# A third place for the low parts of layer 0's queries, and layer 1's attention with its low value product last, its loads asked for one head ahead, and its side work begun earlier

## The chip, the cores and the metric

The kernel runs on one core of one Trainium2 chip. The metric is the device time of one execution in microseconds (us). Five engines work beside each other, each with its own queue of instructions, and they wait for each other by semaphores: PE (TensorE, matrix products; its weight loads are listed apart as PEld), ACT (ScalarE), DVE (VectorE), POOL (GpSimd) and SP (SyncE), which here issues every DMA.

## The reference

The reference is a trunk of two layers over 2048 tokens of width 1024, batch 1, in float32.

- **Layer 0** normalises, multiplies by one combined input matrix and runs two attentions: mixer A (8 query heads and 2 key heads of width 64, a window of own plus two previous 64-token chunks, a learned sink, rotary) and mixer B (8 heads of width 64, own plus eight previous chunks, a learned relative bias). Each output is multiplied by a SiLU gate; both are joined, go through one output matrix and are added to the residual.
- **Layer 1** normalises, multiplies by one input matrix (queries, keys, values, gate) and runs mixer C, differential attention: 8 heads, each with two query and key maps of width 64 and values of width 128, causal by 64-token chunk:

```
s1 = q1 @ k1.T / 8 ; s2 = q2 @ k2.T / 8          # masked by chunk
a  = softmax(s1) - lam * softmax(s2)
o  = a @ v                                       # then RMSNorm per head, SiLU gate, output matrix, residual
```

## The kernel before

**High and low parts.** For its products the kernel splits a float32 operand into a high part H (the rounded copy, made on ACT) and a low part L (what is left, made on DVE or POOL). A product is then three products: H·H, H·L and L·H.

**Four stages.** `project(0)` and `project(1)` make queries, keys, values (and layer 0's gates) and write their parts to scratch tensors in HBM. `mix0` and `mix1` run attention and output projection and load what they need from there. In the profile, layer 0's projection fills about the first 605 us, `mix0` lasts to about 1207, layer 1's projection to 1790.7, and `mix1` to the end.

**Layer 0's attention (`mix0`, names with m).** For each head and block of 512 tokens `load_q` (L524 to L534) brings the high part of a head's queries into a tile `qd` and the low part into `ql`, each with two DMAs of 64 rows. `qd` has three places in SBUF, `ql` two (the default of the pool `ld`, L510). A score is two products in a row (L567 with `qd`, L568 with `ql`).

**Layer 1's attention (`mix1`, names with c).** `heads()` goes through blocks b = 3, 2, 1, 0 of 512 query tokens and in each through 8 heads. For one head and block:

- `load` (L995) brings the keys of the b + 1 blocks, two tiles each (`k0`, `k1`, one for each map m of the differential pair; DMAs at L1002 and L1003), and the values (`vH`, `vL`, L1009). Keys and values have 4 places each, just enough for the 4 blocks of one head at b = 3.
- `scores` (L851) loads the queries (L859, L860) and makes four rows of 128 queries (j = 0 to 3). A row has, for each map m and each stretch z of up to 512 keys, one chunk: two products (L878 with `qd`, L879 with `ql`), a maximum on DVE (L882) and an exponential on ACT (L885). Then POOL scales both maps and joins them (L898 to L912; every fifth join is on DVE).
- `values` (L915) transposes the joined chunks (L925), splits them into H (ACT, L928) and L (DVE, L929), and adds three products into one PSUM tile: vH·H (L932), vH·L (L933), vL·H (L934).
- `gate` ends the head.

Beside the heads runs `side()`: first the gate projection `gates()` (32 tiles of 8 steps, one step being the three products of L214 to L216 called "cG", with weights loaded at L1034), which also reloads the hidden block for the next block of tokens (L1040, L1041), then the output projection ("com").

**What sets the order.** `pace` (L48) writes the program: score chunks and value products in turn, and side steps so that their count follows a table, `STAGES1` (L93): pairs of (units of work done, side steps done), with straight lines between. The program is then ordered by the framework's scheduler, which simulates the engines and may place an instruction earlier than the program names it, when its inputs and a place for its output are free; a DMA may so be issued well ahead of the line that names it. What results is one fixed order for each engine. SP's order matters most for loads: a DMA whose place isn't free yet holds up all DMAs behind it.

Of the kernel before, what the change touches and what calls it, by code (L numbers as in the profile page):

```python
# [11 lines left out]
F32R = mybir.dt.float32r  # L12
# [6 lines left out]
P = 128  # L19
# [3 lines left out]
NTB = 4  # L23
BLK = NTB * P
# [7 lines left out]
def f32(ap):  # L32
    return ap.bitcast(F32)
# [52 lines left out]
class Trunk:  # L86
# [418 lines left out]
    def _mix0(self, es):  # L505
# [18 lines left out]
        def load_q(H, L, h, b, res):  # L524
            tok = slice(b * BLK, (b + 1) * BLK)
            e = h % 2
            r = slice(e * HD, (e + 1) * HD)
            qd = ld.tile([P, BLK], F32R, tag="qd", name=n + "qd", bufs=3)
            nc.sync.dma_start(f32(qd[0:HD, :]), s[H][h // 2, r, tok])
            nc.sync.dma_start(f32(qd[HD:P, :]), s[H][h // 2, r, tok])  # L530
            ql = ld.tile([P, BLK], F32R, tag="ql", name=n + "ql")
            nc.sync.dma_start(f32(ql[0:HD, :]), s[L][h // 2, r, tok])
            nc.sync.dma_start(f32(ql[HD:P, :]), s[L][h // 2, r, tok])
            res["q"] = (qd, ql)  # L534
# [292 lines left out]
    def _mix1(self, es):  # L827
# [20 lines left out]

        count = [0]

        def scores(h, b, K, res):  # L851

            tok = slice(b * BLK, (b + 1) * BLK)
            qd = ld.tile([P, 2, BLK], F32R, tag="qd", name=n + "qd")
            ql = ld.tile([P, 2, BLK], F32R, tag="ql", name=n + "ql")
            for m in range(2):
                r = slice(m * HD, (m + 1) * HD)
                for part, q in (("qH", qd), ("qL", ql)):
                    nc.sync.dma_start(f32(q[0:HD, m, :]), s[part][h, r, tok])  # L859
                    nc.sync.dma_start(f32(q[HD:P, m, :]), s[part][h, r, tok])  # L860
            us = res["u"] = []
            for j in range(NTB):
                t = b * NTB + j
                nk = (t + 1) * P
                cuts = [(c, min(nk, c + 512)) for c in range(0, nk, 512)]
                nb = len(cuts)
                js = slice(j * P, (j + 1) * P)
                nm, la, e = small("nm", 8), small("la", 8), small("e", 8)
                nm, la, e = (x.rearrange("p (m z) -> p m z", m=2) for x in (nm, la, e))
                l, rl = small("l", 2), small("rl", 2)  # L870
                rows = []
                for m in range(2):
                    chunks = []
                    for z, (c, ce) in enumerate(cuts):
                        wd = ce - c
                        ps = pS.tile([P, 512], F32, tag="S", name=n + "S")[:, :wd]
                        kt = K[z][m]
                        mm(ps, qd[:, m, js], kt[:, :wd], start=True, stop=False)  # L878
                        self.anchor = mm(ps, ql[:, m, js], kt[:, :wd], start=False, stop=True).ins  # L879
# [5 lines left out]
                        nc.scalar.activation(chunks[z][:, :wd], ps, AF.Exp, bias=nm[:, m, z:z + 1], accum_out=acc)  # L885
                        yield wd / 256
                    rows.append(chunks)
                if nb > 1:
                    top, pe = small("top", 2), small("pe", 8).rearrange("p (m z) -> p m z", m=2)[:, :, :nb]
                    nc.vector.tensor_reduce(top, nm[:, :, :nb], AX.X, ALU.min)  # L890
                    for m in range(2):
                        nc.scalar.activation(e[:, m, :nb], nm[:, m, :nb], AF.Exp, bias=top[:, m:m + 1], scale=-1.0)
                    nc.vector.tensor_tensor(pe, e[:, :, :nb], la[:, :, :nb], ALU.mult)
                    nc.vector.tensor_reduce(l, pe, AX.X, ALU.add)
                nc.vector.reciprocal(rl, l)
                cs = small("cs", 8).rearrange("p (m z) -> p m z", m=2)
                if nb > 1:
                    nc.gpsimd.tensor_scalar(cs[:, 0, :nb], e[:, 0, :nb], rl[:, 0:1], 1.0, ALU.mult, ALU.mult)  # L898
                    nc.gpsimd.tensor_scalar(cs[:, 1, :nb], e[:, 1, :nb], rl[:, 1:2], self.nlam, ALU.mult, ALU.mult)
                else:  # L900
                    nc.gpsimd.tensor_scalar(cs[:, 1, 0:1], rl[:, 1:2], self.nlam, 1.0, ALU.mult, ALU.mult)
                for z, (c, ce) in enumerate(cuts):
                    p1, p2 = (rows[m][z][:, :ce - c] for m in range(2))
                    c1 = cs[:, 0, z:z + 1] if nb > 1 else rl[:, 0:1]
                    c2 = cs[:, 1, z:z + 1]
                    nc.gpsimd.tensor_scalar(p1, p1, c1, 1.0, ALU.mult, ALU.mult)  # L906
                    count[0] += 1
                    if count[0] % self.COMB == 0:
                        nc.vector.scalar_tensor_tensor(p1, p2, c2, p1, ALU.mult, ALU.add)
                    else:  # L910
                        nc.gpsimd.tensor_scalar(p2, p2, c2, 1.0, ALU.mult, ALU.mult)  # L911
                        nc.gpsimd.tensor_tensor(p1, p1, p2, ALU.add)  # L912
                us.append(rows[0])

        def values(h, b, V, res):  # L915
            us = res["u"]
            O = pO.tile([P, BLK], F32, tag="O", name=n + "O")
            nkt = (b + 1) * NTB
            for kt in range(nkt):
                j0 = max(0, kt - b * NTB)  # L920
                wd = (NTB - j0) * P
                tp = ptr.tile([P, 512], F32, tag="tr", name=n + "tr")
                kk = (kt % 4) * P
                for j in range(j0, NTB):
                    nc.tensor.transpose(tp[:, (j - j0) * P:(j - j0 + 1) * P], us[j][kt // 4][:, kk:kk + P], self.ident)  # L925
                H = sb.tile([P, 512], F32R, tag="ptH", name=n + "ptH", bufs=3)
                L = sb.tile([P, 512], F32R, tag="ptL", name=n + "ptL", bufs=3)
                nc.scalar.activation(H[:, :wd], tp[:, :wd], AF.Copy)  # L928
                nc.vector.tensor_tensor(L[:, :wd], tp[:, :wd], f32(H[:, :wd]), ALU.subtract)  # L929
                o = O[:, j0 * P:]  # L930
                vH, vL = (v[:, kk:kk + P] for v in V[kt // 4])
                mm(o, vH, H[:, :wd], start=(kt == 0), stop=False, skip_group_check=True)  # L932
                mm(o, vH, L[:, :wd], start=False, stop=False, skip_group_check=True)  # L933
                mm(o, vL, H[:, :wd], start=False, stop=(kt == nkt - 1), skip_group_check=True)  # L934
                if kt == 2:
                    while normal:
                        normal.pop(0)()
                yield wd / P
            gate(h, b, O)
# [52 lines left out]
                    split(h, b, o)  # L992
                    yield 1

        def load(h, i, K, V):  # L995

            tok = slice(i * BLK, (i + 1) * BLK)
            ks = []
            for m in range(2):
                k = kp.tile([P, BLK], F32R, tag=f"k{m}", name=n + f"k{m}")  # L1000
                r, o = slice(m * HD, (m + 1) * HD), slice((1 - m) * HD, (2 - m) * HD)
                nc.sync.dma_start(f32(k[r, :]), s["kH"][h, r, tok])  # L1002
                nc.sync.dma_start(f32(k[o, :]), s["kL"][h, r, tok])  # L1003
                ks.append(k)
            K.append(ks)
# [7 lines left out]
            V.append(vs)  # L1013

        room = self.last_hidden
        ended = set()
# [91 lines left out]
        at = [NB - 1]  # L1108

        def heads():  # L1110
            for b in reversed(range(NB)):
                at[0] = b
                for h in range(8):
                    K, V = [], []
                    for i in range(b + 1):
                        load(h, i, K, V)
                    res = {}
                    yield from scores(h, b, K, res)
                    queue.append(values(h, b, V, res))
            queue.append(leave())  # L1120

        def leave():
# [59 lines left out]
```

## Time and profile before

| what | value |
|---|---|
| median of 3 runs | 2928.43 us (2926.35 to 2938.07) |
| the profiled execution's own time | 2935.29 us |
| its span, first to last instruction | 2933.5 us |
| mean granted TensorE clock | 0.972 |
| busy: PE, DVE, POOL, ACT | 93%, 66%, 55%, 54% of the span |
| layer 0's projection | 0 to about 605 us |
| `mix0` | about 605 to 1207 us |
| layer 1's projection | 1207 to 1790.7 us |
| `mix1` | 1790.7 to 2933.5 us |

A busy share says how long an engine had work in it. A product of 512 columns is shown as 0.39 us of busy PE, though at full clock the next one can start 0.23 us after it, so a PE that looks busy is not PE at its peak. The column PEclk of a stretch is the share of full clock that TensorE was granted, and the number in parentheses behind PE is the number of products that ran in it.

### The profile page before, as it was taken

The numbers are of one execution on the slowest core, as the hardware profiler recorded it, in microseconds if no ns is written. First come the engines' busy times: TensorE is split into PE (matmuls) and PEld (weight loads), VectorE is DVE, ScalarE is ACT, GpSimd is POOL, SyncE is SP. The second block draws the span as 40 slices with busy tenths as digits, with TensorE's granted clock in tenths as the row PEclk, the third lists the DMA queues.
The fourth block names the chain that finished last, engine by engine and source line by source line (L and its number), as shares of the span: only waits on it lengthen the run. The fifth ranks groups of instructions, "written<-read, shape, count | busy, mean of one in ns | idle before, by whom it ended". The sixth has DMA issues, their size and how long they took to land.

```text
span 2933.5 us, 45206 instructions
## 1 busy us (share of the span) xinstructions
PE 2726.8 (93%) x13704; PEld 2243.6 (76%) x13704; DVE 1937.4 (66%) x4685; ACT 1595.9 (54%) x4135; POOL 1610.5 (55%) x1968
## 2 busy tenths in 40 slices
PE   7999999998999999999999997889999999898898
PEld 5878888886887887777888885767777777677667
DVE  7752385256788885698548832656657888888742
ACT  4443543367676664334343322657657777777752
POOL 3541251246344443367646631767767778888851
PEclk9999999999999999999999998999999999999999
DMA  4673343649887764567884454585867777668863
GB/s 149 224 249 128 116 144 122 196 145 245 218 205 172 191 176 123 193 209 258 271 288 129 130 176 148 165 233 164 248 180 217 203 226 216 181 182 220 209 216 115
DMA packets 408866, 555.83 MB, mean 189 GB/s; under 512 B 47152, under 2 KB 187184, under 8 KB 408624
## 3 DMA queue, kind: packets, MB, share of 16 engines
q1 hardware_dynamic: 408624, 552.96, 64.1%
q8 instruction: 109, 1.79, 0.3%
q14 instruction: 133, 1.09, 0.1%
HBM read 388.18 MB, written 164.63 MB: 188 GB/s over the span
## 4 chain that ended last, share of the span: by engine, by line
PE 64%; DMA 11%; DVE 11%; ACT 4%; issue 2%; POOL 2%; SPq 1%; DVEq 0%; ACTq 0%; POOLq 0%
PE p1mm L216 4%; PE p1mm L214 4%; PE p1mm L215 4%; PE cS L878 3%; PE cS L879 3%; PE ctr L925 3%; PE p0mm L214 2%; PE p0mm L215 2%; PE p0mm L216 2%; PE cG L214 2%; PE cG L215 2%; PE cG L216 2%; PE cO L933 2%; PE mom L214 2%; PE com L214 2%
## 5 line engine op out<-in xcount | busy, mean ns | idle before, releaser
L885 ACT ACTIVATE cP<-cS,cnm 128x512 f32<-128x512 f32 (+3 forms) x640 | 398.4, 629 | 183.0 <-DVE cnm L882 104.3
L882 DVE TENSOR_REDUCE cnm<-cS 128x1 f32<-128x512 f32 (+3 forms) x640 | 373.6, 600 | 105.9 <-PE cS L879 100.6
L878 PE MATMUL cS<-ck,cqd 128*128 128x512 f32 (+3 forms) x640 | 265.7, 420 | 56.4 <-ACT cP L885 19.7
L304 POOL TENSOR_TENSOR p0wL<-p0ws,p0wH 128x512 fp32r<-128x512 f32 (+1 forms) x128 | 155.5, 1246 | 274.3 <-ACT p0wH L303 264.9
L214 PE MATMUL p1mm<-p1wH,p1hH 128*128 128x512 f32 x768 | 301.8, 394 | 0.8 <-ACT p1wH L303 0.8
L215 PE MATMUL p1mm<-p1wL,p1hH 128*128 128x512 f32 x768 | 301.8, 393 | 0.4 <-POOL p1wL L304 0.4
L216 PE MATMUL p1mm<-p1wH,p1hL 128*128 128x512 f32 x768 | 301.9, 394 | 0.0
L912 POOL TENSOR_TENSOR cP<-cP,cP 128x512 f32<-128x512 f32 (+3 forms) x256 | 284.7, 1132 | 0.4
L304 POOL TENSOR_TENSOR p1wL<-p1ws,p1wH 128x512 fp32r<-128x512 f32 x128 | 167.9, 1331 | 137.1 <-ACT p1wH L303 117.6
L214 PE MATMUL p0mm<-p0wH,p0hH 128*128 128x512 f32 (+1 forms) x640 | 238.1, 375 | 3.4 <-ACT p0vt L454 2.9
L879 PE MATMUL cS<-ck,cql 128*128 128x512 f32 (+3 forms) x640 | 238.1, 377 | 2.9 <-DMA cql<-qL 2.9
L216 PE MATMUL p0mm<-p0wH,p0hL 128*128 128x512 f32 (+1 forms) x640 | 238.2, 373 | 0.1
L215 PE MATMUL p0mm<-p0wL,p0hH 128*128 128x512 f32 (+1 forms) x640 | 238.2, 373 | 0.0
L929 DVE TENSOR_TENSOR cptL<-ctr,cptH 128x512 fp32r<-128x512 f32 (+1 forms) x320 | 190.5, 599 | 62.9 <-ACT cptH L928 62.1
L928 ACT ACTIVATE cptH<-ctr 128x512 fp32r<-128x512 f32 (+1 forms) x320 | 169.9, 539 | 64.8 <-PE ctr L925 63.5
L878 PEld LDWEIGHTS cS<-ck,cqd 128*128 128x128 f32 x640 | 124.6, 195 | 98.4 <-ACT cP L885 45.7
L906 POOL TENSOR_SCALAR cP<-cP,ccs 128x512 f32<-128x512 f32 (+3 forms) x288 | 188.9, 672 | 0.0
L925 PE MATMUL ctr<-ident,cP 128*128 128x128 f32 x1088 | 175.5, 277 | 0.6 <-POOL cP L912 0.3
L898 POOL TENSOR_SCALAR ccs<-ce,crl 128x4 f32<-128x4 f32 (+2 forms) x96 | 26.9, 280 | 270.1 <-ACT cP L885 130.1
L911 POOL TENSOR_SCALAR cP<-cP,ccs 128x512 f32<-128x512 f32 (+3 forms) x256 | 173.6, 691 | 0.0
L215 PEld LDWEIGHTS p1mm<-p1wL,p1hH 128*128 128x128 f32 x768 | 144.8, 189 | 29.8 <-POOL p1wL L304 0.8
L214 PEld LDWEIGHTS p1mm<-p1wH,p1hH 128*128 128x128 f32 x768 | 144.7, 189 | 29.7 <-ACT p1wH L303 1.0
(325 smaller groups left out, 7873.8 us busy)
## 6 DMA issues: line engine op xcount, KB each, us to landing
p1ws<-in_od_w_in_dram SPq DMA_DIRECT2D x56, 512.0 KB, 4.8
p0ws<-in_ev_w_in_dram SPq DMA_DIRECT2D x48, 512.0 KB, 4.2
ck<-kH SPq DMA_DIRECT2D x160, 128.0 KB, 4.0
ck<-kL SPq DMA_DIRECT2D x160, 128.0 KB, 4.2
cvH<-vH SPq DMA_DIRECT2D x80, 256.0 KB, 3.8
cvL<-vL SPq DMA_DIRECT2D x80, 256.0 KB, 4.5
cqd<-qH SPq DMA_DIRECT2D x128, 128.0 KB, 4.9
cql<-qL SPq DMA_DIRECT2D x128, 128.0 KB, 4.8
```

Source lines behind the costliest of these rows:

```text
L214: mm(ps, aH, bH, start=first, stop=False)
L215: mm(ps, aH, bL, start=False, stop=False)
L216: mm(ps, aL, bH, start=False, stop=last)
L304: nc.gpsimd.tensor_tensor(l[:, :width], ws[:, k, :width], f32(h[:, :width]), ALU.subtract)
L878: mm(ps, qd[:, m, js], kt[:, :wd], start=True, stop=False)
L879: self.anchor = mm(ps, ql[:, m, js], kt[:, :wd], start=False, stop=True).ins
L882: nc.vector.tensor_reduce(nm[:, m, z:z + 1], ps, AX.X, ALU.max, negate=True)
L885: nc.scalar.activation(chunks[z][:, :wd], ps, AF.Exp, bias=nm[:, m, z:z + 1], accum_out=acc)
L906: nc.gpsimd.tensor_scalar(p1, p1, c1, 1.0, ALU.mult, ALU.mult)
L912: nc.gpsimd.tensor_tensor(p1, p1, p2, ALU.add)
L925: nc.tensor.transpose(tp[:, (j - j0) * P:(j - j0 + 1) * P], us[j][kt // 4][:, kk:kk + P], self.ident)
L929: nc.vector.tensor_tensor(L[:, :wd], tp[:, :wd], f32(H[:, :wd]), ALU.subtract)
```

## The change

Three edits, as they stand in the diff:

1. In `mix0` the tile `ql` gets three places instead of two.
2. In `values` of `mix1` the product with the low part of the probabilities (vH·L) goes from second to third place.
3. In `mix1` the loads are named elsewhere in the program. Queries are loaded by `load_q`, keys by `load_k` (one tile at a time) and values by `load_v`. For the first head, queries are named first and then the keys, map 0 for all blocks, then map 1. For every other head a callback `then(j, m, z)`, called behind each exponential, names the queries in row j = 2 of the head before, a key tile behind the chunk of row j = 3 that last reads the place it takes, and the values of the head's own block z in its row j = 3 of map 0.

Beside these, `STAGES1` gets one point more: (32, 45), so that 45 side steps are due at 32 units, where the straight line from (0, 0) to (600, 288) gave 15.

```diff
-    STAGES1 = ((0, 0), (600, 288), (780, 360), (1000, 440), (1088, 520))
+    STAGES1 = ((0, 0), (32, 45), (600, 288), (780, 360), (1000, 440), (1088, 520))
...
-            ql = ld.tile([P, BLK], F32R, tag="ql", name=n + "ql")
+            ql = ld.tile([P, BLK], F32R, tag="ql", name=n + "ql", bufs=3)
...
                 mm(o, vH, H[:, :wd], start=(kt == 0), stop=False, skip_group_check=True)
-                mm(o, vH, L[:, :wd], start=False, stop=False, skip_group_check=True)
-                mm(o, vL, H[:, :wd], start=False, stop=(kt == nkt - 1), skip_group_check=True)
+                mm(o, vL, H[:, :wd], start=False, stop=False, skip_group_check=True)
+                mm(o, vH, L[:, :wd], start=False, stop=(kt == nkt - 1), skip_group_check=True)
...
-            for b in reversed(range(NB)):
+            order = [(h, b) for b in reversed(range(NB)) for h in range(8)]
+            q, K = load_q(*order[0]), {(i, m): load_k(0, i, m) for m in range(2) for i in range(NB)}
+            for (h, b), nxt in zip(order, order[1:] + [None]):
                 at[0] = b
-                for h in range(8):
-                    K, V = [], []
-                    for i in range(b + 1):
-                        load(h, i, K, V)
-                    res = {}
-                    yield from scores(h, b, K, res)
-                    queue.append(values(h, b, V, res))
+                after, res = [None, {}], {"v": []}
+
+                def then(j, m, z):
+                    if (j, m, z) == (2, 0, 0) and nxt:
+                        after[0] = load_q(*nxt)
+                    if j == NTB - 1:
+                        if nxt and z <= nxt[1]:
+                            after[1][z, m] = load_k(nxt[0], z, m)
+                        if m == 0:
+                            res["v"].append(load_v(h, z))
+
+                yield from scores(h, b, q, K, res, then)
+                queue.append(values(h, b, res))
+                q, K = after
```

No product, tile or DMA is added or taken away; what changes is where they stand. Three places in the built orders show it.

**SP, where layer 1's projection ends and `mix1` begins.** `vH` and `vL` stores (L467, L468) write the projection's last values; cvH and cvL are the first head's values, cqd and cql its queries. Its keys stand further up in both orders. Before:

```order
L1009 DMA cvH_20918<-vH_74 128x4x128
L1009 DMA cvL_20920<-vL_75 128x4x128
L467 DMA vH_74<-p1vH_20860 128x512
L468 DMA vL_75<-p1vL_20861 128x512
L1009 DMA cvH_20928<-vH_74 128x4x128
L1009 DMA cvL_20930<-vL_75 128x4x128
L1009 DMA cvH_20938<-vH_74 128x4x128
L1009 DMA cvL_20940<-vL_75 128x4x128
L1009 DMA cvH_20948<-vH_74 128x4x128
L1009 DMA cvL_20950<-vL_75 128x4x128
L859 DMA cqd_20952<-qH_70 64x512
L860 DMA cqd_20952<-qH_70 64x512
```

Now:

```order
L858 DMA cqd_20912<-qH_70 64x512
L859 DMA cqd_20912<-qH_70 64x512
L467 DMA vH_74<-p1vH_20860 128x512
L468 DMA vL_75<-p1vL_20861 128x512
L858 DMA cql_20913<-qL_71 64x512
L859 DMA cql_20913<-qL_71 64x512
```

The eight value loads have left the stretch ahead of the queries; the first two query loads stand ahead of the projection's last stores. The value loads now stand sixteen rows behind the last of these, after the second head's queries and eight loads of gate weights.

**SP, the keys of the second head of `mix1`.** ck0 is map 0, ck1 map 1; the numbers rise with the block z. Before, the last rows of the group, where block 3 of map 0 (ck0_21361) stands behind three tiles of map 1:

```order
L1002 DMA ck0_21351<-kH_72 64x512
L1003 DMA ck0_21351<-kL_73 64x512
L1002 DMA ck1_21334<-kH_72 64x512
L1003 DMA ck1_21334<-kL_73 64x512
L1002 DMA ck1_21344<-kH_72 64x512
L1003 DMA ck1_21344<-kL_73 64x512
L1002 DMA ck1_21354<-kH_72 64x512
L1003 DMA ck1_21354<-kL_73 64x512
L1002 DMA ck0_21361<-kH_72 64x512
L1003 DMA ck0_21361<-kL_73 64x512
```

Now, from block 1 of map 0 on:

```order
L1006 DMA ck0_21337<-kH_72 64x512
L1007 DMA ck0_21337<-kL_73 64x512
L1040 DMA cwH_21444<-wgH_82 128x512
L1006 DMA ck0_21360<-kH_72 64x512
L1007 DMA ck0_21360<-kL_73 64x512
L1006 DMA ck0_21377<-kH_72 64x512
L1007 DMA ck0_21377<-kL_73 64x512
L1053 DMA g1_76<-cgt_21387 128x512
L1006 DMA ck1_21396<-kH_72 64x512
L1007 DMA ck1_21396<-kL_73 64x512
```

All of map 0 stands ahead of map 1 now, and one load of gate weights (cwH) and one store of a gate tile (g1) stand between the keys, where the group held keys alone.

**SP in `mix0`.** mqd and mql are the two parts of a head's queries; a and b in aqH, bqH name the mixer. Before:

```order
L530 DMA mqd_7919<-aqH_57 64x512
L586 DMA mgt_7604<-g0_67 128x512
L539 DMA mks_7991<-bkH_64 64x1024
L540 DMA mks_7991<-bkL_65 64x1024
L681 DMA mbias_7996<-in_relb_dram 128x256
L676 DMA mvB_7546<-bv_66 128x4x128
L529 DMA mqd_7985<-bqH_62 64x512
L532 DMA mql_7922<-aqL_58 64x512
```

Now:

```order
L529 DMA mqd_7919<-aqH_57 64x512
L530 DMA mqd_7919<-aqH_57 64x512
L532 DMA mql_7922<-aqL_58 64x512
L760 DMA g0_67<-mgt_7563 128x512
L533 DMA mql_7922<-aqL_58 64x512
L539 DMA mks_7991<-bkH_64 64x1024
```

The low part of the same head (mql_7922) stood six rows behind the second half of its high part (mqd_7919), behind keys, a bias, values and the next head's high part; it now stands right behind it.

On PE, the built orders also show the new point of the table: when the first head's last score product is issued, 13 gate steps stand ahead of it before, and 36 now; at the end of the second head 38 and 62, of the third 63 and 80.

More of the change, by code (lines that the diff above doesn't have):

```diff
@@ L849, in _mix1, with load_q @@
         count = [0]
-        def scores(h, b, K, res):
+        def load_q(h, b):
             tok = slice(b * BLK, (b + 1) * BLK)
@@ L860, in scores @@
                     nc.sync.dma_start(f32(q[HD:P, m, :]), s[part][h, r, tok])
+            return qd, ql
+        def scores(h, b, q, K, res, then):
+            qd, ql = q
             us = res["u"] = []
@@ L913, in scores, with values @@
                 us.append(rows[0])
-        def values(h, b, V, res):
+        def values(h, b, res):
             us = res["u"]
@@ L993, in fetch, with load_k, load_v @@
                     yield 1
-        def load(h, i, K, V):
+        def load_k(h, i, m):
             tok = slice(i * BLK, (i + 1) * BLK)
[L998 to L1005, printed above, removed]
+            k = kp.tile([P, BLK], F32R, tag=f"k{m}", name=n + f"k{m}")
+            r, o = slice(m * HD, (m + 1) * HD), slice((1 - m) * HD, (2 - m) * HD)
+            nc.sync.dma_start(f32(k[r, :]), s["kH"][h, r, tok])
+            nc.sync.dma_start(f32(k[o, :]), s["kL"][h, r, tok])
+            return k
+        def load_v(h, i):
+            tok = slice(i * BLK, (i + 1) * BLK)
             vs = []
@@ L1012, in load @@
                 vs.append(v)
-            V.append(vs)
+            return vs
         room = self.last_hidden
```

5 lines of the change are left out of this document (3 added, 2 removed).

## The prediction

> **What bounds the kernel now.** I read the waits of PE first, because the page shows it 93% busy, then stretches of the four stages, then the timeline at the places that the change touches.
>
> ```profile
> PE cO L933 <- DVE cptL L929: 22.3, 21, 3.9
> PE cS L878 <- ACT cP L885: 19.7, 34, 4.6
> PE cS L878 <- DMA cql<-qL: 14.6, 2, 13.3
> PE mSA L568 <- DMA mql<-aqL: 12.5, 6, 3.6
> PE cS L878 <- DMA ck<-kL: 8.5, 5, 4.6
> PE cS L878 <- DMA cvH<-vH: 7.6, 1, 7.6
> PE mSB L568 <- DMA mql<-bqL: 4.2, 4, 2.2
> PE cS L878 <- ACT csq L951: 3.4, 1, 3.4
> ```
>
> Columns are total us, times, longest us. Every edit has a row here: the order of the value products (L933), queries and keys in layer 1 (L878), low parts of queries in layer 0 (L568). Without the row for ACT, which no edit touches, they are 73 us, 2.5% of the run.
>
> ```profile
> 720.00:1165.00 445.00, 410.43 (x2497) 357.60 (x2496) 340.99 (x1139) 285.85 (x743) 200.79 (x288) 0.97 0.71 183
> 1790.00:1865.00 75.00, 50.35 (x178) 36.75 (x178) 36.67 (x76) 32.67 (x96) 35.80 (x50) 0.78 0.65 186
> 1865.00:2470.00 605.00, 571.41 (x2802) 456.49 (x2801) 431.68 (x935) 413.76 (x1141) 448.40 (x603) 0.98 0.73 210
> 2470.00:2933.50 463.50, 412.49 (x1955) 323.63 (x1953) 312.83 (x782) 292.98 (x814) 320.94 (x468) 0.94 0.67 184
> 1784.84 0.39 PE L216 MATMUL p1mm<-p1wH,p1hL 128*128 128x512 f32 x1
> 1785.07 0.39 PE L214 MATMUL p1mm<-p1wH,p1hH 128*128 128x512 f32 x1
> ```
>
> The columns of a stretch are length, busy time of PE, PEld, DVE, ACT, POOL, then granted clock, DMA share, GB/s. PE has the most work in each, and DVE, ACT and POOL have a quarter or more of their time left in the third, where the first and second blocks' heads run beside the gate projection. The first 75 us of `mix1` are the weak place: 178 products, which at 0.23 us from start to start (last two rows) need 41 us, in 75. So the kernel is bound by PE with holes, and the holes are latency: things that arrive late at an engine that takes them in order.
>
> **The change part by part.** The sum is made against the profiled execution's own 2935.3 us (span 2933.5, 1.8 around it). That execution is 6.9 us above the median of the runs, so 6.9 comes off at the end.
>
> *A, the entry to `mix1`.*
>
> ```profile
> 1791.75 0.46 SPq L467 DMA_DIRECT2D vH<-p1vH  x1
> 1792.30 0.38 SPq L468 DMA_DIRECT2D vL<-p1vL  x1
> 1797.08 0.69 SPq L1009 DMA_DIRECT2D cvL<-vL  x1
> 1798.11 0.54 SPq L859 DMA_DIRECT2D cqd<-qH  x1
> 1799.97 0.59 SPq L860 DMA_DIRECT2D cql<-qL  x1
> 1804.00 1.73 PE L878 MATMUL cS<-ck,cqd 128*128 128x512 f32 x4 [13.33 <-DMA cql<-qL]
> 1806.09 1.72 PE L879 MATMUL cS<-ck,cql 128*128 128x512 f32 x4 [0.36 <-DMA cql<-qL]
> cql<-qL SPq DMA_DIRECT2D x128, 128.0 KB, 4.8
> 1805.00:1810.00 5.00, 3.71 (x10) 2.56 (x9) 2.29 (x5) 2.26 (x8) 0.00 (x0) 0.50 0.91 295
> ```
>
> PE's last projection product starts at 1790.3; then it waits 13.3 us, because SP issues eight value loads (the last at 1797.1) and only then the queries. In the new order two query loads go out before the last stores, and the low part right behind them: the stores' 1792.3 + 0.4, two issues of 0.6, and 4.8 us to land (page) give 1798.7 at the latest for the second products, against 1806.1. The stores themselves can leave up to half a us earlier without value loads ahead. **A = -8**, from -6 (landing as slow as the 6.1 us from 1799.97 to 1806.09) to -13 (the whole gap). Half clock follows (last row, 0.50); I leave it in, since 5 us of idle remain. The Trainium skill ("TensorE: Matmul & The Clock Gate", "Part 1: The HAM clock gate") puts the fall to half clock at one idle window of about 3.4 us; the trace agrees, 0.50 after 13.33 us of idle. By that rule a remaining idle shorter than the window would spare the fall too and A would be about -10; the sum keeps -8.
>
> *B, the first head.* The new point of the table puts 36 instead of 13 gate steps ahead of the first head's last score, so 23 steps of three products, 23 x 3 x 0.23 = 16 us of PE work.
>
> ```profile
> 1819.80 0.27 POOL L898 TENSOR_SCALAR ccs<-ce,crl 128x4 f32<-128x4 f32 x1 [74.29 <-ACT cP L885]
> 1850.09 0.27 POOL L898 TENSOR_SCALAR ccs<-ce,crl 128x4 f32<-128x4 f32 x1
> 1855.34 3.72 POOL L912 TENSOR_TENSOR cP<-cP,cP 128x512 f32<-128x512 f32 x3
> ```
>
> The head's four rows leave POOL at a pace of 10 us (1819.8 to 1850.1 for three), the last at 1859; values can't start before. PE has 75 - 41 = 34 us free in the stretch, 13 of them the entry, so 21 for these 16: they fit and are hidden. What they save comes later, where the same 16 us are missing from a stretch in which PE is busy 571 of 605 us. By the third head 17 steps of lead are left (12 us). The bounds are -16 (PE sets the pace throughout) and 0 (the later heads are paced by something else). I take **B = -10**, nearer the first, as PE is the fullest engine there.
>
> *C, key loads from head to head.* A key tile's place frees when row j = 3 has read it, and row j = 0 of the next head asks for it eight chunks later.
>
> ```profile
> SPq L1009 <- PE cO L934: 70.4, 30, 7.7
> SPq L1002 <- PE cS L879: 51.1, 46, 6.9
> 2156.27 0.37 SPq L1009 DMA_DIRECT2D cvH<-vH  x1
> 2160.03 0.45 SPq L1002 DMA_DIRECT2D ck<-kH  x1
> 1955.00:1960.00 5.00, 0.00 (x0) 0.00 (x0) 0.00 (x0) 0.00 (x0) 5.00 (x5) 0.53 1.09 249
> 1960.00:1965.00 5.00, 4.40 (x10) 3.47 (x11) 0.69 (x1) 2.12 (x6) 0.50 (x1) 0.50 1.02 226
> 2175.00:2180.00 5.00, 4.04 (x12) 3.20 (x13) 1.67 (x7) 2.27 (x5) 1.90 (x4) 0.50 0.52 155
> 2180.00:2185.00 5.00, 5.00 (x15) 3.94 (x14) 2.40 (x3) 1.56 (x4) 5.00 (x7) 0.60 0.56 176
> ```
>
> SP waits 70 us with a value load whose place the last head's products still hold, and keys stand behind it (third and fourth row). The waits of L878 for ck and cvH, and the one put down to csq, which I count as a late key too, are 8.5 + 7.6 + 3.4 = 19.5 us; the half clock behind the two long ones costs PE half of its busy time at 0.50 (2.2 + 2.0) and 2.0 at 0.60: 26 us in all. Map 0's last block now goes ahead of map 1, in the order in which the scores use the tiles. What remains is the wait at 1953: there the DMA share is 1.09, keys, values and the reloaded hidden block all come at once, and no order of 9 MB makes them fewer. That is 7.6 + 2.2 = 10 us. **C = -16**; bounds -26 (all) and +10 (one more such collision, as the gate steps that carry the reload move). The Trainium skill ("DMA: Bandwidth & Descriptors", "Specifications") gives about 358 GB/s as HBM's limit for a core; here the engines are full at 249 GB/s, so the trace doesn't agree that there is room. By the page all 26 us could go, and the sum would be 10 us lower.
>
> *D, the low product last.* In 21 waits L933 stood for cptL; with vL·H ahead of it, 0.23 us of each are covered: 4.8 us. Long waits (3.9) keep the rest. **D = -5**, bounds 0 (another row of DVE is late instead) and -10 (as many again too short to be listed, hidden in the 0.39 us that a product is shown busy).
>
> *E, `mix0`.*
>
> ```profile
> 695.99 1.02 SPq L530 DMA_DIRECT2D mqd<-aqH  x1
> 700.53 0.55 SPq L532 DMA_DIRECT2D mql<-aqL  x1
> 709.35 0.51 PE L568 MATMUL mSA<-mksA,mql 128*128 128x256 f32 x1 [3.41 <-DMA mql<-aqL]
> 710.00:715.00 5.00, 5.00 (x28) 4.57 (x27) 3.13 (x9) 2.10 (x6) 4.56 (x8) 0.71 0.70 208
> ```
>
> Here is the stall whole: the low part leaves 4.5 us behind the high part, PE stands 3.4 us between the two products, and the clock is 0.71 behind it. With a third place both leave together, so this wait goes. The page's waits for mql are 12.5 + 4.2 = 16.7; half clock adds some 3 (two or three such, 1.5 each). Against it: what stood ahead of mql, keys and biases, is now behind it, and the DMA share is 0.71 on average. **E = -9**, about half; bounds -20 and 0.
>
> Sum: -8 - 10 - 16 - 5 - 9 = **-48 us**: 2935.3 - 48 = 2887.3 for an execution like the profiled one, less 6.9 gives **2880 us**.
>
> **The rivals.**
>
> *1. Loads are limited by the 16 DMA engines, not by order.* For it: shares of 1.09 and 1.02 above, and the first head now asks for 23/8 = 3 more gate tiles' weights in the same time. Against: the mean share is 0.73. Then C is 0, E -4, B -5: -8 - 5 - 0 - 5 - 4 = -22, **2906 us**.
>
> *2. Slower: gate weights hold up keys.*
>
> ```profile
> SPq L1034 <- PE cG L216: 125.4, 36, 12.1
> ```
>
> A load of gate weights waits for PE to use up the tile before it, up to 12.1 us. In the new order one stands inside the second head's key group, where none stood. If that holds at each of the seven head boundaries of block 3, each costs what the one at 1953 cost, 10 us: 70 instead of 26, C = +44, B is lost, and -8 + 0 + 44 - 5 - 9 = +22, **2950 us**. It decides from about five such boundaries on (26 + 22 = 48). Against: keys are named earlier than before, and their places, not the weights, were what they waited for (51 us).
>
> *3. Slack.* What PE no longer waits for loads, it waits for the softmax: the row of 19.7 us for ACT grows. For it: POOL is at 448 of 605 us, with a pace of 10 us a row that the change doesn't touch. Then B and C are 0, E -4, D -2: -8 - 4 - 2 = -14, **2914 us**, at the edge of what can be told.
>
> **How the numbers follow.** A measurement of this kernel tells about 0.5% from no change, 14.6 us (2913.8 and 2943.1). Forecast 0.53, with its own range 2855 to 2900; rival 1 0.25; rival 3 0.15; rival 2 0.07. Faster: 0.53, most of rival 1 (0.21) and a quarter of rival 3 (0.04): 0.78. Same: the rest of both, 0.14. Slower 0.08. For the range, the lower end takes A to D at their best and E near it, -13 - 16 - 26 - 10 - 14 = -79 (2935.3 - 79 - 6.9 = 2849), and a little for bounds set too near: 2845; the upper end holds rivals 1 and 3: 2920.
>
> **What would show it.** A: the first product of L883 within 3 us of the last projection product, L884's wait for cql under 8 us, POOL's first L898 (now L904) before 1813. B: 178 products in the first 75 us become 220 or more. C: L883's waits for ck below 5 us in total and SP's wait for cO L940 well below 70. D: the wait for cptL, then at L940, near 17. E: L568's waits for mql below 6 us, `mix0` shorter by about 9. Wrong it would be if L883's waits for ck or ACT grow by what the loads give up, if SP's wait at L1040 grows past 150 us, or if `mix0` keeps its 602 us with mks in the place of mql.

## The result, and the profile after

The changed kernel takes **2905.99 us** (median of 4 runs, 2904.72 to 2908.11) against 2927.64 for the kernel before beside it: ratio 0.9911, 95% interval 0.9892 to 0.9931, about -26 us (-20 to -32; the two medians themselves lie 21.7 us apart). A second measurement on another occasion gave 2907.16 and 0.9908 (0.9886 to 0.9930). The kernel is faster, then, by about half of what was forecast (-48).

The profiled execution took 2905.8 us (span 2903.8), 29.5 less than that of before. The waits of PE after the change (line, producer and its line, total us, times, longest us; L883 was L878, L940 stands where L933 stood):

```profile
PE cS L883 <- ACT cP L890: 19.0, 29, 2.4
PE cS L883 <- DMA ck<-kL: 16.4, 11, 3.4
PE cO L940 <- DVE cptL L935: 15.8, 14, 4.0
PE mSA L567 <- ACT mPA L622: 7.6, 7, 2.1
PE cS L884 <- DMA cql<-qL: 6.9, 5, 2.0
PE mSB L567 <- ACT mPA L622: 6.1, 4, 2.6
PE ctr L931 <- DVE cP L915: 3.7, 1, 3.7
PE mSA L568 <- DMA mql<-aqL: 2.1, 2, 1.1
```

Three things changed as meant: the wait for cql went from 14.6 to 6.9 us, that for cptL from 22.3 to 15.8, that for mql from 16.7 to 2.1. Three did not. The rows that the prediction counts as late keys read 19.5 us in all before (8.5 for ck, 7.6 for cvH, 3.4 for csq); the last two are gone, but ck now reads 16.4, and a smaller row for the keys' high part (kH) 1.2, so keys are as late as they were. `mix0` waits for ACT's mPA instead of its queries, and a wait that the profile of before doesn't have stands in the seventh row.

The stretches answer to those shown of before (length, busy us of PE, PEld, DVE, ACT, POOL, granted clock, DMA share, GB/s):

```profile
1790.00:1865.00 75.00, 67.16 (x278) 52.52 (x277) 35.69 (x77) 35.05 (x100) 36.38 (x50) 0.91 0.81 239
1865.00:2470.00 605.00, 570.63 (x2824) 459.58 (x2823) 455.02 (x973) 428.31 (x1180) 463.46 (x626) 0.97 0.74 208
```

The first 75 us hold 278 products where they held 178. The next 605 us hold 22 more than before, at a clock of 0.97 against 0.98: the first head's gain is kept, and little is added to it.

To say where the time went I cut `mix1` at ACT's copies of each head's finished result (`cot`, L955, 32 of them) and count from the last projection product. One profiled execution of each kernel, in us:

| kernel | first head ends | 7 more of block 3 | block 2 | block 1 | block 0 and rest | `mix1` | `mix0` |
|---|---|---|---|---|---|---|---|
| before | 113.1 | 383.1 | 296.2 | 195.2 | 155.6 | 1143.2 | 601.9 |
| changed | 105.3 | 363.7 | 295.1 | 193.7 | 150.7 | 1108.5 | 605.7 |
| changed, second time | 107.0 | 363.3 | 293.8 | 200.9 | 150.7 | 1115.8 | 601.9 |

So `mix1` gave 27 to 35 us, most of it in block 3's eight heads (-27.2 and -25.9), and `mix0` none. Single executions of one order scatter by some 7 to 13 us over all of `mix1` (two kernels below whose `mix1` orders are identical read 1123.4 and 1110.2), and `mix0` by as much; a single stretch or a single stall scatters less. Verdicts below rest on the timed ratios.

### The profile page after: what moved, and what is told of

The parts are those of the page before. It is cut to its first block, busy times and chain, and to the rows that moved or that the text cites. A ratio compares the mean times of both kernels' runs of the same rounds, so it can differ in the third digit from the quotient of the medians.

```text
span 2903.8 us, 45243 instructions
## 1 busy us (share of the span) xinstructions
PE 2718.9 (94%) x13704; PEld 2244.2 (77%) x13704; DVE 1950.6 (67%) x4685; ACT 1597.0 (55%) x4135; POOL 1612.4 (56%) x1968
## 4 chain that ended last, share of the span: by engine, by line
PE 71%; DVE 11%; DMA 10%; ACT 4%; issue 2%; POOL 1%; SPq 1%; DVEq 0%; ACTq 0%; POOLq 0%
PE p1mm L216 5%; PE p1mm L214 5%; PE p1mm L215 5%; PE p0mm L214 3%; PE p0mm L215 3%; PE p0mm L216 3%; PE cS L883 3%; PE cS L884 3%; PE ctr L931 3%; PE cG L214 2%; PE cG L216 2%; PE cG L215 2%; PE cO L940 2%; PE com L214 2%; PE com L215 2%
## 5 line engine op out<-in xcount | busy, mean ns | idle before, releaser
L883 PE MATMUL cS<-ck,cqd 128*128 128x512 f32 (+3 forms) x640 | 264.5, 417 | 42.4 <-ACT cP L890 19.0
L918 POOL TENSOR_TENSOR cP<-cP,cP 128x512 f32<-128x512 f32 (+3 forms) x256 | 285.1, 1135 | 0.3
L883 PEld LDWEIGHTS cS<-ck,cqd 128*128 128x128 f32 x640 | 124.7, 195 | 83.1 <-ACT cP L890 42.3
L917 POOL TENSOR_SCALAR cP<-cP,ccs 128x512 f32<-128x512 f32 (+3 forms) x256 | 170.6, 679 | 0.0
L216 PEld LDWEIGHTS p1mm<-p1wH,p1hL 128*128 128x128 f32 x768 | 145.8, 190 | 29.1 <-issue 0.2
```

The source lines that it names most:

```text
L216: mm(ps, aL, bH, start=False, stop=last)
```

## The experiments

Each ratio is against the kernel before, run beside it. Ratios are turned into us with 2930, so an interval of 0.002 to each side is 6 us to each side.

### The four parts alone

**Third place alone** (only `bufs=3` for `ql` in `mix0`).

> The kernel before with the third place for layer 0's low query parts alone. The prediction: -9 us, by waits of PE for mql gone. The reading of the changed kernel's trace: those waits go (16.7 to about 2 us) but PE waits for the softmax and the output projection's low parts instead, and layer 0's attention is 4 us longer: +2 to +5 us. Layer 1's attention is as before within 2 us in both.

Measured: 0.9995 (0.9976 to 1.0015), nothing. Its waits in `mix0`:

```profile
PE mSB L567 <- ACT mPA L622: 6.9, 4, 3.3
PE mSA L567 <- ACT mPA L622: 5.0, 7, 1.4
PE mSA L568 <- DMA mql<-aqL: 4.0, 3, 1.9
PE mSB L568 <- DMA mql<-bqL: 2.8, 1, 2.8
```

Before:

```profile
PE mSB L567 <- ACT mPA L622: 3.0, 3, 2.2
PE mSA L567 <- ACT mPA L622: 1.2, 2, 0.6
```

The waits for mql fell from 16.7 to 6.8 us and those for mPA rose from 4.2 to 11.9: the softmax of the chunk before was almost as late as the queries. In the fourteen profiles of this case `mix0` reads 597.2 to 611.8 with the third place (8 executions, mean 605.3) and 597.1 to 607.3 without (6, mean 603.1).

**Low product last alone** (the two lines in `values` exchanged).

```diff
-                mm(o, vH, L[:, :wd], start=False, stop=False, skip_group_check=True)
-                mm(o, vL, H[:, :wd], start=False, stop=(kt == nkt - 1), skip_group_check=True)
+                mm(o, vL, H[:, :wd], start=False, stop=False, skip_group_check=True)
+                mm(o, vH, L[:, :wd], start=False, stop=(kt == nkt - 1), skip_group_check=True)
```

> The kernel before with the low value product last alone. The prediction: -5 us, by 0.23 us of each of 21 waits. A rival: each small change of the program lets the scheduler place thousands of instructions elsewhere, and this is worth more, in either sign, than the 5 us: then the time is more than 5 us away from -5.

Measured: 0.9966 (0.9948 to 0.9985), -10 us (-4 to -15), in the middle twice the forecast. The wait for cptL:

```profile
PE cO L934 <- DVE cptL L929: 15.3, 12, 3.6
```

It fell by 7.0 us, from 21 times to 12; block 2, which has 13.9 of these 22.3 us before and 9.6 now, is 10 us shorter (286.1 against 296.2). So there the wait itself makes 4.3 of the 10. The expectation's rival, that the scheduler places other instructions elsewhere too, is not excluded: in the two traces at least 1178 of the 4928 products of `mix1` stand elsewhere in PE's order, where the exchange itself moves 320, and the new point alone (next), with a wait for cptL of 21.5 us, makes block 2 shorter by 6.7 us as well.

**New point of the table alone** ((32, 45) in `STAGES1`).

> The kernel before with the point (32, 45) of the side table alone. The prediction: -10 us, from gate steps moved into the first head. A rival: the gain needs the early start of the first head by the loads' order, since before it PE stands still for loads, not for lack of gate steps; the gate weights are loaded behind the queries; then 0 to -4 us.

Measured: 0.9976 (0.9959 to 0.9993), -7 us (-2 to -12) for a forecast of -10. The first stretch in its profile:

```profile
1790.00:1865.00 75.00, 57.52 (x240) 45.92 (x239) 32.41 (x72) 33.79 (x97) 36.38 (x50) 0.86 0.76 223
```

62 products more in the first 75 us, and the first head ends where it did (113.8 against 113.1): the steps filled idle time, as foreseen.

**New loads alone** (`load_q`, `load_k`, `load_v` and `heads()` as changed; the rest as before).

> The changed loads of layer 1 alone (queries first for the first head, the others named one head ahead), without the other three edits. The prediction: A and C, -8 - 16 = -24 us. The rival of limited DMA engines: A alone, -8 to -10 us, and waits for ck of 15 us as in the changed kernel.

Measured: 0.9940 (0.9922 to 0.9958), -17.6 us, where A and C together were put at -24. The next run parts the two.

**The entry alone.** The kernel before, where only the first head names queries, then keys, then values:

```diff
+                    if (h, b) == (0, NB - 1):
+                        q = load_q(h, b)
+                        for i in range(b + 1):
+                            load_k(h, i, K)
+                        for i in range(b + 1):
+                            load_v(h, i, V)
+                    else:
```

> The kernel before, with one thing changed: for the first head of layer 1 the queries are asked for first, then all key tiles, then all value tiles; every other head loads as before. This is term A alone. The new loads as a whole (A and C) measured -17.6 us (ratio 0.9940), forecast -24. Theory (A and C are separate stalls that add): a_entry is about -8 us, ratio 0.9973, the first layer-1 score comes within 5 us of the last projection product (before 13.7), and C is what is left, -9 to -10. Rival (slack: what the entry gains the first heads give back to the softmax, POOL's pace of 10 us a row): the entry is shorter by 8 to 10 us but the first head's last copy-out is not earlier, ratio 0.998 or above, and then nearly all of the -17.6 belongs to the later heads' keys.

Measured: 0.9947 (0.9929 to 0.9964), -15.5 us. That is all but 2 of the 17.6 that the new loads gave (the two intervals make that difference uncertain by some 7), so the forecast's split of them was wrong: the entry (A) is worth twice its -8, the head-to-head keys (C) next to nothing as they come out. Its first products:

```profile
1788.29 1.52 PE L881 MATMUL cS<-ck,cqd 128*128 128x512 f32 x4 [3.88 <-issue]
1794.32 1.73 PE L882 MATMUL cS<-ck,cql 128*128 128x512 f32 x4 [4.50 <-DMA cql<-qL]
```

The one gap of 13.3 us became two, 3.9 and 4.5, and the second products start 10.3 us behind the last projection product instead of 15.8. The first head ends 12.3 us earlier (100.8 against 113.1), and the later heads keep it, so the rival that the softmax takes it back falls.

### One part taken out of the whole

**Without the third place.**

> The changed kernel without the third place for low parts of queries in layer 0 (one argument undone). Alone that place measured 0.9995 [0.9976, 1.0015]. Theory (E is worth nothing, because the low part's wait gives way to a wait of the next products for the softmax and for keys): same time as the changed kernel within 4 us, 2902 to 2910, with the wait for mql back at some 15 us in all and the wait of mSA and mSB for ACT smaller by as much. Rival (the place costs a little in the whole, since mix0 of the changed kernel reads 605.7 against 601.9): faster than the changed kernel by 4 to 6 us, about 2900. Second rival (E as forecast): slower by 9 us, about 2915.

Measured: 0.9924 (0.9908 to 0.9939), against 0.9911 and 0.9908 with it: no difference that can be told, as expected. Its waits for mql are back (16.4 us) and those for mPA small again (1.6).

**Without the new point.**

> The changed kernel without the new point (32, 45) of the gate's table. Alone the point measured -7 us (0.9976). Theory (parts share the same late softmax in the first blocks, and overlap): without it the changed kernel is slower by 3 to 7 us, 2909 to 2913, the first 75 us of mix1 hold about 190 products instead of 278, and the wait of L883 for ACT's cP grows. Rival (parts add): slower by 7 to 10 us, 2913 to 2916. Second rival (with the entry mended the point does nothing): 2906.

Measured: 0.9880 (0.9861 to 0.9899), *faster* than the changed kernel. All three expectations missed.

**With the old order of the value products.**

> The changed kernel with the value products in the old order (vH.H, vH.L, vL.H). Alone the new order measured -10 us (0.9966), twice the forecast 5. Theory (the order covers 0.23 us at each of some 20 to 40 products that stand for cptL, wherever loads are): slower by 5 us, about 2911, with the wait for cptL near 22 us in some 20 times. Rival (in the whole the order gains as much as alone): slower by 10 us, 2916, and part of it is fewer falls to half clock. Second rival (its gain is the same slack that the loads use up): 2906 to 2908.

Measured: 0.9882 (0.9865 to 0.9899), faster too, and again all three missed. So each of the two parts, worth 7 to 10 us alone, costs some 8 us in the whole. The next two runs ask whether that was the chip's luck: the changed kernel once more, beside the kernel that has neither.

> The changed kernel itself once more, beside the runs it is compared with, since differences of 0.3% are at stake. Expected: the ratio of the first measurement, 0.9911, within its interval. Theory (the new point of the gate's table and the new order of the value products each cost a little in the whole): its time is above that of loads_ql3, which has neither, and stays near 0.991. Rival (the 0.9880 and 0.9882 of the two kernels that lack one of them were the chip's luck): it comes out at 0.988 as they did.

> The changed kernel without the new point of the gate's table and with the value products in the old order: only the new loads of layer 1 and the third place in layer 0. With one of the two parts the whole measured 0.9880 and 0.9882, with both 0.9911, the new loads alone 0.9940. Theory (each of the two is worth some 10 us as long as the other is absent, because both fill the same holes of the first block): 0.994 again, as the loads alone. Rival (neither is worth anything once the loads are in order): 0.988, 9 us below the changed kernel.

Measured: 0.9908 (0.9886 to 0.9930) for the changed kernel again, and 0.9939 (0.9916 to 0.9962) with neither. The first number repeats, so the rival of luck falls for the changed kernel; and the kernel with neither is not faster than it, as the theory of the first of these two expectations had it, but as slow as the new loads alone (0.9940), as the theory of the second had it. With the new loads and the third place throughout:

| | old product order | low product last |
|---|---|---|
| old table | 0.9939 | **0.9880** |
| new point | **0.9882** | 0.9911, 0.9908 |

Either part is worth some 17 us on top of the loads; the second then costs 8. Each of these steps is uncertain by 7 to 9 us, so the cost of 8 is at the edge of what the intervals tell; that the two don't add (-17 and -17 alone, -9 together) is beyond it. The two fastest kernels that leave nothing out, 2900.67 and 2899.35 us, are the changed one with either part undone.

**What the second part costs.** One place where it loses time is the second head of block 2. From the copy of one head's result to that of the next, in the changed kernel, and then in the one with the old product order:

```profile
2297.53:2340.12 42.59, 37.58 (x183) 30.51 (x181) 37.02 (x70) 28.87 (x82) 33.65 (x45) 0.92 0.66 184
```

```profile
2292.52:2326.90 34.38, 34.38 (x179) 28.33 (x178) 28.06 (x63) 27.29 (x78) 29.66 (x41) 1.00 0.72 203
```

Both stretches have 48 gate and 36 value products on PE. The second runs without a hole at full clock; the first is 8.2 us longer. The timeline of PE shows how it begins:

```profile
2297.68 0.40 PE L884 MATMUL cS<-ck,cql 128*128 128x512 f32 x1
2301.79 0.69 PE L931 MATMUL ctr<-ident,cP 128*128 128x128 f32 x2 [3.71 <-DVE cP L915]
...
2302.70 0.63 PE L214 MATMUL cG<-p1hH,cwH 128*128 128x512 f32 x1
2303.13 0.63 PE L215 MATMUL cG<-p1hL,cwH 128*128 128x512 f32 x1
```

PE stands 3.7 us at a transposition whose chunk DVE is still joining, with gate products, which wait for nothing when their turn comes, queued behind it. Afterwards they start every 0.43 us instead of 0.23: half clock, 6.8 us in the clock's records, which is 3.4 us lost. With a later idle of 1.0 us that makes 8.1 of the 8.2. All four profiles with loads, point and new order have this wait, at the same instruction and 3.70 to 3.73 us long; none of the other ten has it. In block 2 as a whole the profiles agree: with exactly one of the two parts 286.0 to 289.5 us (5 kernels), with both 293.8 to 298.1, with neither 293.8 to 300.1. The orders of the engines are fixed when the program is built, so this stall is built into the order that the two parts give together. That it is the whole of the loss was not tried, and it is not likely: by the clock's records PE lost 44.4, 46.1 and 45.1 us to half clock over all of `mix1` in the three complete kernels that have both parts and the new loads, 28.2 and 32.8 in the two with one of them, 36.6 and 39.3 in the two with neither. These are single executions, and those of the two kernels with one part are the fastest of their kernels (2888.14 and 2892.62 us), so the sizes are uncertain.

### The hidden block's loads left out

A long wait for keys at each of three places in the changed kernel:

```profile
1903.40 0.47 PE L883 MATMUL cS<-ck,cqd 128*128 128x512 f32 x1 [2.46 <-DMA ck<-kL]
...
2061.33 0.77 PE L883 MATMUL cS<-ck,cqd 128*128 128x512 f32 x1 [3.39 <-DMA ck<-kL]
...
2212.46 0.77 PE L883 MATMUL cS<-ck,cqd 128*128 128x512 f32 x1 [2.55 <-DMA ck<-kL]
```

The DMA engines there (share is the number before the last, GB/s the last):

```profile
1900.00:1905.00 5.00, 2.54 (x11) 1.76 (x10) 2.70 (x7) 3.54 (x10) 1.55 (x2) 0.91 1.12 280
2055.00:2060.00 5.00, 1.15 (x8) 0.89 (x8) 0.56 (x4) 2.45 (x7) 0.00 (x0) 0.77 1.01 247
2205.00:2210.00 5.00, 2.75 (x18) 2.25 (x18) 2.77 (x8) 3.16 (x10) 4.81 (x5) 1.00 1.10 221
```

And what SP issues ahead of the first of the three:

```profile
1895.47 0.58 SPq L1046 DMA_DIRECT2D p1hH<-hH  x1
1896.10 0.43 SPq L1047 DMA_DIRECT2D p1hL<-hL  x1
1897.18 0.45 SPq L1006 DMA_DIRECT2D ck<-kH  x1
1897.97 0.45 SPq L1007 DMA_DIRECT2D ck<-kL  x1
```

Each time, the next block's hidden tiles (16 loads of 256 KB within 18 to 31 us) go out between or just ahead of the keys at a head's end, with the engines full. The experiment leaves these loads out, in the changed kernel and in the one without the new point. Both compute the gates of blocks 2, 1 and 0 with block 3's hidden tiles:

```diff
-                        if c == 7 and b:
-                            before = slice((b - 1) * BLK, b * BLK)
-                            nc.sync.dma_start(f32(hH), s["hH"][k, :, before])
-                            nc.sync.dma_start(f32(hL), s["hL"][k, :, before])
-                        elif c == 7:
+                        if c == 7 and not b:
```

> The changed kernel, but the gate's hidden block is not loaded again for the second to fourth block (the gates are computed with the first block's; 48 loads of 256 KB, 12.6 MB, are left out, and no others). In the changed kernel's trace the waits for ck at 1901, 2054 to 2061 and 2206 to 2212 lie at the three places where these loads go out, with the DMA engines' share at 1.0 to 1.1. Theory (the keys are late because the engines are full there): L883's waits for ck fall from 16.4 us to below 6, the three falls to half clock behind them go, and the time falls by 12 to 22 us, 2884 to 2894. Rival (keys are late because their places come free only eight chunks ahead, or because SP stands at a gate weight or a value load): waits for ck stay at 12 us or more and the time is within 5 us of the changed kernel.

> The same leaving out of the hidden block's loads, but without the new point of the gate's table. In the changed kernel the point moves these loads to 1880 to 1905, 2025 to 2060 and 2180 to 2200, each onto the end of a head, where the next head's keys and this head's values are loaded; without it they lie at 1918 to 1945, 2058 to 2075 and about 2200 to 2215. Theory (the point's 23 early steps are worth their 7 to 10 us, and lose them to this collision): without these loads the point pays again, so this kernel is 5 to 10 us slower than after_no_reload. Rival (the steps fill no hole once the entry is mended, they only push the first head back): this kernel is as fast as after_no_reload or up to 10 us faster.

Measured: 0.9865 (0.9844 to 0.9887) and 0.9853 (0.9830 to 0.9875). The changed kernel gains 15.3 us beside its own second measurement (2891.81 against 2907.16; 12.6 by the two ratios), within the 12 to 22 expected. PE's order in `mix1` is nearly kept, with 53 of 4928 products elsewhere, so a new order hardly explains the gain. The waits and the stretch in it:

```profile
PE cS L883 <- DMA ck<-kL: 9.2, 11, 2.1
```

```profile
1865.00:2470.00 605.00, 578.89 (x2894) 466.64 (x2893) 471.06 (x1006) 438.57 (x1215) 481.65 (x647) 0.99 0.68 192
```

The total stays above the 6 us expected because 5.3 of the 9.2 lie in blocks 1 and 0; up to 2470 us it is 3.9 against 13.5. The seven later heads of block 3 take 345.7 us instead of 363.7, so the gain lies where these loads are. The keys are late because of these 12.6 MB of other loads. The engines' shares of 1.0 and more speak for their bytes as the reason; but the 48 places that they take in SP's queue went with them, so the two are not told apart. Neither the release of the keys' places, which is as it was, nor SP standing at a gate weight explains it: SP's wait at L1040 is 96.9 us here, longer than the changed kernel's 83.9. The new point still doesn't pay without these loads (0.9865 with it, 0.9853 without; without it, leaving them out gives 8 us, 0.9880 to 0.9853), so the collision alone does not explain why the point fails in the whole. Both kernels have the low product last, and the one with the point has the wait of 3.7 us in block 2.

## Why the prediction was right or wrong

The direction was right and the time (2906 for 2880) lay in the range, but outside the 2855 to 2900 that the forecast gave itself: it lay where the first rival stood, loads limited by the DMA engines. Point by point:

- **A, entry, -8: right in mechanism, too small.** Alone it measured -15.5 us, 12.3 of them by the end of the first head. In the changed kernel the second products start 7.9 us behind the last projection product, against 15.8 before, which is the -8 (5.5 us of it in the entry alone); the first at 4.2, a little above the "within 3 us". POOL's first L904 stands at 1812.9, just before the 1813 named:

```profile
1795.23 0.39 PE L216 MATMUL p1mm<-p1wH,p1hL 128*128 128x512 f32 x1
1799.45 1.72 PE L883 MATMUL cS<-ck,cqd 128*128 128x512 f32 x4 [3.83 <-issue]
1803.16 1.19 PE L884 MATMUL cS<-ck,cql 128*128 128x512 f32 x2 [1.99 <-DMA cql<-qL]
```

  The mis-sized term is the half clock that I "leave in": with one gap of 13.3 us turned into two short ones, the time lost to it in the first 50 us of `mix1` fell from 13.7 to 8.5 us in the entry alone and to 6.8 in the changed kernel. I had put that at nothing. The rule of the Trainium skill ("TensorE: Matmul & The Clock Gate", "Part 1: The HAM clock gate") that the prediction set beside it, a fall at one idle window of about 3.4 us, agrees with what stayed: the idle left is 3.83 us, and the clock still fell. But the trace doesn't agree that a shorter idle is spared: at the single waits of 2.46 and 2.55 us for keys shown above, the granted clock falls to 0.50 too (1904.2 to 1907.5 and 2211.4 to 2218.0).
- **B, first head, -10: right alone (-7), wrong in the whole.** The early products are there (278, forecast 220 or more). "They fit and are hidden" held only as long as the entry left the first head slow: without the point the first head ends at 96.5 instead of 105.3. The point also moves the hidden block's loads, from 1920 to 1948 back to 1880 to 1906, onto the end of a head.
- **C, keys, -16: wrong.** The failed step is "Map 0's last block now goes ahead of map 1 ... What remains is the wait at 1953". I charged one collision with the hidden block, 10 us, as the one thing that order couldn't mend; there are three hidden blocks to be loaded, and in the changed kernel each meets a head's end. Late keys cost PE 17.6 us there, against the 19.5 that were to shrink. New loads less entry measured about -2 us, uncertain by some 7; the collisions cost the changed kernel 15. The bound of +10, "one more such collision, as the gate steps that carry the reload move", named the mechanism and was not taken. SP's wait with value loads did not fall. The row that was to be well below 70 us, for cO L940, reads 37.7, but only because vL is now last read one product earlier, at L939: both rows together rose from 80.4 to 90.6. Before, with the row of 10.0 that the prediction leaves out, and now:

```profile
SPq L1009 <- PE cO L934: 70.4, 30, 7.7
SPq L1009 <- PE cO L933: 10.0, 3, 3.7
SPq L1015 <- PE cO L939: 52.9, 20, 6.8
SPq L1015 <- PE cO L940: 37.7, 26, 7.4
```

- **D, low product last, -5: right in its sign (-10 alone), wrong in the whole.** The wait for cptL, 15.8, is near the 17 forecast, and it fell by 7.0 alone; that this cover is what gave the -10 is not shown, since the order changed elsewhere too. What was missing is that the reordered program as a whole may hold a new stall, as it does together with B.
- **E, third place, -9: wrong.** "With a third place both leave together, so this wait goes": the wait went, the time did not. What was late next was the softmax of the chunk before (mPA, 4.2 to 13.7 us in the changed kernel), and I had looked only among loads for what would be late next.
- **The sum.** Alone, the parts measured -1.5, -10, -7 and -17.6, -36 together; the whole is -26. Adding terms was itself a step, and it failed. The 10 us between these sums are within their joint uncertainty (some 12), but the table of the two parts shows it: B and D each cost about 8 us once the other is there.
- **The rivals.** The first (DMA engines) gave the time and its mechanism is shown for C, though not its sizes for E and B: A and D were larger alone, E nothing, and B a loss in the whole. That its sum of -22 comes so near is luck. The second (gate weights hold up keys) did not happen; SP's wait there fell from 125.4 to 83.9 us. The third (softmax) holds in `mix0` alone; in `mix1` the wait for ACT stayed (19.7 to 19.0).

What stays open: why each of B and D measures 17 us on top of the new loads and only 7 to 10 on top of the kernel before. On top of the loads, block 2 is some 8 us shorter with exactly one of them than with neither (286.0 and 286.2 against 293.8), which is less than half of the 17.

## What to carry to other kernels

When a change mends the order of loads, list every other load that is tied to the same clock of work, and ask where it moves: the keys here were late because 12.6 MB of other loads came at a head's end, although the change names the keys earlier. When a scheduler writes the order, the gains of parts measured alone are no terms of a sum; undo each part within the whole, since one of them may now cost. A wait that goes is worth only its distance to the next thing that is late at the same instruction.

## What the runs showed of the hardware that was not expected

**DVE stands for POOL.** The join behind the 3.7 us wait, on DVE and then on POOL at the same time:

```profile
2296.62 5.11 DVE L915 SCALAR_TENSOR_TENSOR cP<-cP,ccs,cP 128x512 f32<-128x512 f32 x1
2301.66 0.41 DVE L887 TENSOR_REDUCE cnm<-cS 128x1 f32<-128x256 f32 x1
```

```profile
2295.37 2.03 POOL L912 TENSOR_SCALAR cP<-cP,ccs 128x512 f32<-128x512 f32 x3
2297.39 1.35 POOL L917 TENSOR_SCALAR cP<-cP,ccs 128x512 f32<-128x512 f32 x2
2298.71 2.47 POOL L918 TENSOR_TENSOR cP<-cP,cP 128x512 f32<-128x512 f32 x2
```

The instruction takes 0.93 us in the median of all 64, 46 of them of this width; here it stays open 5.11, until POOL's unbroken chain ends (2298.71 + 2.47 = 2301.18) and 0.55 more. In the four executions that have this place it reads 5.10 to 5.12. The Trainium skill ("SBUF — State Buffer", "Who interferes with whom") says that a DVE instruction with two inputs from SBUF contends with a POOL instruction that reads SBUF, and that the ports which they share are an exclusive lock. The trace agrees that one waits (5.11 us instead of 0.93), and shows more: DVE stood through the last four POOL instructions in a row (two of L917, two of L918), not through one. That this is the cause was not tested by an experiment.

**The DMA engines are full at very different rates.** Shares of 1.01 to 1.12 stand beside 221 to 280 GB/s in the three stretches above, so the rate at which they are full cannot be told from one stretch.
